# Twenty blocks of weight sums formed in the mixer, kept in DRAM, and read by the second feed-forward

## The chip, the core and the metric

The kernel runs on one core of one Trainium2 chip. The metric is the time of one execution on the device in microseconds (us); of several executions the median is taken. The engines are named as the profile names them: PE is TensorE (matrix products), with PEld its weight loads; DVE is VectorE; ACT is ScalarE; POOL is GpSimd; SP is SyncE, which computes nothing here and issues DMA transfers. A "q" behind a name (SPq, PEq) is that engine's instruction queue.

## The reference

One decoder layer over 256 tokens of width 2048 in float32: a feed-forward, a token mixer, a cross-attention into 256 memory rows, a second feed-forward, a final norm.

```python
def swiglu(h, w_gate, w_up, w_down):
    return (jax.nn.silu(h @ w_gate) * (h @ w_up)) @ w_down

for l in range(DEPTH):                                   # DEPTH = 1
    x = x + 0.5 * swiglu(rms_norm(x, ffn1_norm[l]), ffn1_w_gate[l], ffn1_w_up[l], ffn1_w_down[l])
    x = gated_parallel_mixer(x, mix_norm[l], w_in[l], ...)   # windowed attention beside RWKV-7
    x = memory_cross_attention(x, mem, cross_norm[l], ...)
    x = x + 0.5 * swiglu(rms_norm(x, ffn2_norm[l]), ffn2_w_gate[l], ffn2_w_up[l], ffn2_w_down[l])
return rms_norm(x, final_norm)
```

The weights of a feed-forward are 2048 x 5632 (gate, up) and 5632 x 2048 (down); each is read from DRAM once. The mixer's input projection is 2048 x 8992.

## The kernel before, in words

**Precision.** Each float32 operand is split into a high part `hi` (a rounding copy on ACT) and the rest `lo` (a subtraction on DVE). One product of 128 rows x 128 deep x 512 columns is then three matmuls on PE: hi x hi, hi x lo, lo x hi (`times`, lines 413 to 415 of the profile). Activations are split once; weights are split as they stream in, on lines 339 (`hi`) and 340 (`lo`) in `split_unit`.

**Order of the weights.** `weight_plan` lists all weights in the order of their use. A unit is two rows of 128 (KU = 2) by 512 columns of one weight, 512 KB. An item is what PE takes in one go: one unit, or, in the feed-forwards, a pair of units (gate and up, or two column blocks of down). In the feed-forwards one DMA brings two units of a weight (1 MB, tile `raw2`, four buffers); in the mixer each brings one (tile `raw`, four buffers). All weight loads are issued by SP, in order; a load waits on SP until the buffer that it overwrites has been read. `next_item` loads several units ahead and splits (`divide`) one pair, or two single units, ahead. `hi` and `lo` have three buffers each.

**Seven products.** A pair item multiplies two token halves by two weights over two rows of 128: eight products, 24 matmuls. For the pairs listed in `SEVEN` (pairs 0, 2, 4 of the eight in each column block of gate and up) a scheme of the Strassen and Winograd kind needs seven products, 21 matmuls. It needs sums: four of activations, made once (`combinations`), and four of weights, made for each such item in `sums`, by four subtractions on DVE (lines 350 to 353) from the raw gate and up units, and then split into `thi` (ACT, line 355) and `tlo` (DVE, line 356). `thi` and `tlo` hold all four sums and have one buffer. The four sums lie in two tiles from the `raw` ring until they are split. `product_pair` issues the seven products in the order p1, p2, p7, p6, p4, p3, p5; p6 and p7 go to PSUM banks `tr`, which the transposes share.

**Stages.** The first feed-forward (`feed_forward`, pool `f1`) runs to about 690 us of the profile, the mixer and the cross-attention (pool `mx`) to about 1545 us, the second feed-forward (pool `f2`) to the end. In each feed-forward the 11 column blocks of gate and up come in groups of 4, 4 and 3, each followed by its part of down. The first block of gate and up is plain; ten blocks use seven products. In the mixer, products with `w_in` (`product`) alternate on PE with small work: attention, decay, the recurrence (`pair`, with the masked products `mk` on line 1186) and its finish. That small work is written as Python generators in an `Interleave`; each `tick` of a product advances every group of them a step, so the program's text is woven together. A scheduler that runs when the program is built then fixes the order on each engine by its own estimate of times; on the chip each engine goes through its list in order.

**Where the mixer keeps things.** Most of its tiles share the ring `t4` (N4 = 20 buffers of 4 KB in each partition). The chunks of the recurrence run after the attention branch has been gated; at that point the weights of receptance and value and the second gate are multiplied.

The lines the change touches: the constants near the top, `feed_forward_plan`, the constants `bdup` and `center`, the building of `items`, `load`, `sums`, `divide`, `next_item`, `combinations`, `product_pair`, and the begin of the `mx` pool.

## Time and profile before

| | |
|---|---|
| median of 3 runs (lowest, highest) | 2269.42 us (2266.2, 2269.75) |
| the profiled execution, its own time | 2267.66 us |
| its span, first to last instruction | 2265.9 us |
| mean granted clock of TensorE | 0.999 |
| bytes moved by DMA | 432.75 MB, mean 191 GB/s |
| slices of 1/40 of the span: highest and lowest rate | 262 and 88 GB/s |

The profiled execution is one more execution, read by the hardware profiler. Busy time is the time in which an engine has at least one instruction in work; matmuls overlap, so a busy PE need not be at its full pace, and the distance from one matmul's start to the next says more. "Idle before" is the time an engine stood still before the instructions of a group, put down to whatever ended it. Idle time of an engine that is not the bottleneck costs nothing.

### The profile page before, as it was taken

How to read it: one execution, taken by the hardware profiler on the slowest of the kernel's cores; microseconds unless marked ns; L12 is line 12 of the kernel's file. 1: busy time of each engine (PE TensorE's matmuls, PEld its weight loads, DVE VectorE, ACT ScalarE, POOL GpSimd, SP SyncE). 2: the span in 40 equal slices, each digit the busy share in tenths (PEclk: the TensorE clock that was granted, in tenths of full speed). 3: DMA queues.
4: the chain of work that ended last, by engine and by line, in shares of the span. 5: the costliest groups of instructions: out<-in, count | busy, mean ns of one | idle time of the engine just before them, and what ended most of it. 6: DMA issues, size and time to landing. Idle time of an engine off the chain costs nothing.

```text
span 2265.9 us, 28100 instructions
## 1 busy us (share of the span) xinstructions
PE 2244.2 (99%) x10613; PEld 1840.5 (81%) x10613; DVE 1784.2 (79%) x2283; ACT 1230.7 (54%) x1655; POOL 134.1 (6%) x194
## 2 busy tenths in 40 slices
PE   9999999999999999999999999999999999999998
PEld 7888888888888877788888888888888888888886
DVE  7899989898988477895444556547899998998987
ACT  6555555555556477544444446556555555555554
POOL 1000000000001000201220021001000000000001
PEclk9999999999999999999999999999999999999999
DMA  7565565555556544676533486657555556556563
GB/s 262 186 206 200 189 212 196 186 204 205 187 195 203 164 134 140 195 229 208 150 88 93 154 262 228 195 168 262 202 187 205 203 198 210 186 188 220 186 212 141
DMA packets 219240, 432.75 MB, mean 191 GB/s; under 512 B 14140, under 2 KB 16417, under 8 KB 219105
## 3 DMA queue, kind: packets, MB, share of 16 engines
q1 hardware_dynamic: 210432, 404.78, 54.1%
q0 software_dynamic: 8208, 25.39, 3.5%
q8 instruction: 83, 1.36, 0.2%
q10 hardware_dynamic: 464, 0.79, 0.1%
q14 instruction: 53, 0.43, 0.1%
HBM read 417.56 MB, written 13.11 MB: 190 GB/s over the span
## 4 chain that ended last, share of the span: by engine, by line
PE 86%; DVE 5%; issue 4%; DMA 2%; ACT 2%; POOL 0%; SPq 0%; POOLq 0%; DVEq 0%; ACTq 0%
PE acc L413 17%; PE acc L414 17%; PE acc L415 17%; PE mm L414 7%; PE mm L415 7%; PE mm L413 7%; DVE lo L340 2%; PE tr L600 2%; PE tr L414 2%; PE tr L415 2%; PE tr L413 2%; PE mm L1212 1%; DMA raw<-in_ffn_w_down_dram 1%; PE tr L1181 1%; ACT hi L339 1%
## 5 line engine op out<-in xcount | busy, mean ns | idle before, releaser
L339 ACT CAST hi<-raw 128x1024 fp32r<-128x1024 f32 (+1 forms) x770 | 766.0, 997 | 731.1 <-PE acc L415 423.8
L340 DVE TENSOR_TENSOR lo<-raw,hi 128x1024 fp32r<-128x1024 f32 (+1 forms) x770 | 892.2, 1164 | 341.5 <-ACT hi L339 339.5
L413 PE MATMUL acc<-hi,xhi 128*128 128x512 f32 (+1 forms) x1196 | 476.9, 399 | 3.1 <-ACT xhi L627 2.5
L414 PE MATMUL acc<-lo,xhi 128*128 128x512 f32 (+1 forms) x1196 | 465.8, 389 | 2.2 <-DVE lo L340 2.0
L415 PE MATMUL acc<-hi,xlo 128*128 128x512 f32 (+1 forms) x1196 | 464.6, 389 | 0.0
L413 PEld LDWEIGHTS acc<-hi,xhi 128*128 128x128 f32 x1196 | 224.7, 188 | 52.5 <-issue 5.1
L414 PEld LDWEIGHTS acc<-lo,xhi 128*128 128x128 f32 x1196 | 224.9, 188 | 49.9 <-DVE lo L340 4.4
L415 PEld LDWEIGHTS acc<-hi,xlo 128*128 128x128 f32 x1196 | 224.4, 188 | 47.6 <-DVE xlo L628 1.0
L355 ACT CAST thi<-raw 128x1024 fp32r<-128x1024 f32 x172 | 180.4, 1051 | 102.3 <-DVE raw L351 55.1
L356 DVE TENSOR_TENSOR tlo<-raw,thi 128x1024 fp32r<-128x1024 f32 x172 | 208.9, 1221 | 4.5 <-ACT thi L355 4.5
L413 PE MATMUL mm<-hi,xhi 128*128 128x512 f32 x380 | 149.2, 393 | 0.0
L415 PE MATMUL mm<-hi,xlo 128*128 128x512 f32 x380 | 148.1, 390 | 0.0
L414 PE MATMUL mm<-lo,xhi 128*128 128x512 f32 x380 | 148.1, 390 | 0.0
L414 PE MATMUL acc<-lo,hhi 128*128 128x512 f32 x372 | 145.5, 391 | 0.4 <-DVE lo L340 0.4
L415 PE MATMUL acc<-hi,hlo 128*128 128x512 f32 x372 | 145.4, 391 | 0.0
L413 PE MATMUL acc<-hi,hhi 128*128 128x512 f32 x372 | 145.1, 390 | 0.0
L415 PEld LDWEIGHTS mm<-hi,xlo 128*128 128x128 f32 x380 | 71.3, 188 | 15.0
L413 PEld LDWEIGHTS mm<-hi,xhi 128*128 128x128 f32 x380 | 71.4, 188 | 14.5
L414 PEld LDWEIGHTS mm<-lo,xhi 128*128 128x128 f32 x380 | 71.4, 188 | 14.5
L414 PEld LDWEIGHTS acc<-lo,hhi 128*128 128x128 f32 x372 | 69.9, 188 | 14.9 <-DVE lo L340 0.8
L350 DVE TENSOR_TENSOR raw<-raw,raw 128x512 f32<-128x512 f32 x86 | 59.1, 688 | 28.9 <-DMA raw<-in_ffn_w_up_dram 23.7
L413 PEld LDWEIGHTS acc<-hi,hhi 128*128 128x128 f32 x372 | 69.8, 188 | 14.4
(386 smaller groups left out, 3559.1 us busy)
## 6 DMA issues: line engine op xcount, KB each, us to landing
raw<-in_ffn_w_up_dram SPq DMA_DIRECT2D x88, 1024.0 KB, 6.8
raw<-in_ffn_w_down_dram SPq DMA_DIRECT2D x88, 1024.0 KB, 5.5
raw<-in_ffn_w_gate_dram SPq DMA_DIRECT2D x84, 1024.0 KB, 5.3
raw<-in_w_in_dram SPq DMA_DIRECT2D x136, 512.0 KB, 3.8
raw<-in_w_out_dram SPq DMA_DIRECT2D x32, 512.0 KB, 4.7
raw<-in_w_proj_attn_dram SPq DMA_DIRECT2D x16, 512.0 KB, 3.6
raw<-in_w_proj_rwkv_dram SPq DMA_DIRECT2D x16, 512.0 KB, 5.7
raw<-in_w_cross_kv_dram SPq DMA_DIRECT2D x16, 512.0 KB, 3.7
```

Source lines behind the costliest of these rows:

```text
L339: at["hi"] = act.copy(hi[:, s], raw[:, s])
L340: at["lo"] = dve.tensor_tensor(lo[:, s], raw[:, s], f32(hi[:, s]), ALU.subtract)
L350: dve.tensor_tensor(ta[:, 0], ru[:, 0], rg[:, 0], ALU.subtract)
L355: act.copy(hi[:, 2 * i : 2 * i + 2], t[:])
L356: dve.tensor_tensor(lo[:, 2 * i : 2 * i + 2], t[:], f32(hi[:, 2 * i : 2 * i + 2]), ALU.subtract)
L413: pe.matmul(o, xh, hi, start=first, stop=False, **how)
L414: pe.matmul(o, xh, lo, start=False, stop=False, **how)
L415: pe.matmul(o, xl, hi, start=False, stop=last, **how)
L600: pe.transpose(b[:, o : o + P], tok[:, t, col : col + P], ident[:])
L1181: pe.matmul(b[e][:, m * P : (m + 1) * P], x1[r, j, cs_], x2[r, j, cs_], start=True, stop=True,)
L1212: pe.matmul(vb[:, o : o + P][:, r], lhs(e), rhs[:, r], start=first and e == 0, stop=True, **ek,)
```

## The change

1. In the second feed-forward, gate and up take seven products in pairs 0, 1, 2 and 4 of the ten column blocks (`SEVEN_2`), not 0, 2 and 4.
2. The sums of pairs 1 and 2 of those blocks (`STAGED`), 20 items, are not formed there. A new generator, `stage`, runs twice side by side in the mixer. For each item it loads the up and the gate unit by SP into two `t4` tiles, forms the four sums on DVE in place, and stores the two tiles by SP to the DRAM tile `sums_d`. The first four items come at the mixer's beginning (`STAGE_EARLY`); the other 16 after the mark "gated", at the recurrence.
3. `load_sums` brings the sums back into two `raw` tiles, asked for two items ahead. The row of up that is then not needed (`first_unused`) is left out of its load.
4. In both feed-forwards a seven item is split in another order: the first two sums, then gate, the second row of up, and the last two sums. The parts are now `thia`/`tloa` and `thib`/`tlob`, one buffer each. The order of products is now p7, p6, p1, p2, p3, p4, p5.
5. `bdup` and `center` move into the mixer's pool; N4 goes from 20 to 22.

```diff
-N4 = 20
+N4 = 22
+STAGE_EARLY = 4
 SEVEN, SEVEN_DOWN = (0, 2, 4), ((2, 4, 6), (2, 4))
+SEVEN_2, STAGED = (0, 1, 2, 4), (1, 2)
...
-                yield (wg, wu), 0, KD, (j * 512, j * 512), SEVEN
+                yield (wg, wu), 0, KD, (j * 512, j * 512), SEVEN_2 if last else SEVEN
...
+    bg.group("stage", 2)
...
-            items += [((u + i, u + 2 + i), (k - k0) // KU + i in n) for i in range(2)]
-    raws, parts = {}, {}
+            for i in range(2):
+                q = (k - k0) // KU + i
+                if n == SEVEN_2 and q in STAGED:
+                    staged[len(items)] = len(staged)
+                items.append(((u + i, u + 2 + i), q in n))
+    raws, parts, summed = {}, {}, {}
+    first_unused = {items[i][0][1] for i in staged}
+    sums_d = dram.tile([len(staged), P, 4, 512], F32, name="sums")
...
+        if u in first_unused:
+            second = u + 1 in first_unused
+            pieces = [(slice(1, 2), nc.sync)] + [(slice(2 + second, 4), nc.sync)]
+            if not second:
+                pieces = ((slice(1, 4), nc.sync),)
+        elif u + 1 in first_unused and wide:
+            pieces = ((slice(0, 2), nc.sync), (slice(3, 4), nc.sync))
...
+    def load_sums(i):
+        if i not in staged or i in summed:
+            return
+        summed[i] = [
+            wp.tile([P, KU, 512], F32, tag="raw", name="raw", bufs=4) for _ in range(2)
+        ]
+        for e, t in enumerate(summed[i]):
+            nc.sync.dma_start(t[:], sums_d[staged[i], :, KU * e : KU * e + KU, :])
+
+    def stage(t4, first):
+        yield from idle(8 * first)
+        for i, n in list(staged.items())[first::2]:
+            if n >= STAGE_EARLY:
+                yield from wait_for("gated")
+                yield from idle(8 * first * (n < STAGE_EARLY + 2))
+            t = t4("su", (P, KU, 512)), t4("sg", (P, KU, 512))
+            for e, v in zip(t, items[i][0][::-1]):
+                w, k, c0, _ = units[v]
+                rows = slice(k * P, (k + KU) * P)
+                nc.sync.dma_start(e[:], w[rows, c0 : c0 + 512].rearrange("(a p) n -> p a n", p=P))
+            yield from idle(7)
+            u0, u1, g0, g1 = (e[:, c] for e in t for c in range(KU))
+            with tc.issue_after(at["lo"].ins):
+                dve.tensor_tensor(g0, u0, g0, ALU.subtract)
+                dve.tensor_tensor(u0, u1, u0, ALU.subtract)
+            yield
+            with tc.issue_after(at["lo"].ins):
+                dve.tensor_tensor(u1, u1, g0, ALU.subtract)
+                dve.tensor_tensor(g1, g1, u1, ALU.subtract)
+            yield from idle(3)
+            for c, e in enumerate(t):
+                nc.sync.dma_start(sums_d[n, :, KU * c : KU * c + KU, :], e[:])
+            yield from idle(2)
...
-    def sums(g, u):
...
+    def two_parts(v, e):
+        sp = at["pool"]
+        hi = sp.tile([P, KU, 512], F32R, tag="thi" + e, name="thi")
+        lo = sp.tile([P, KU, 512], F32R, tag="tlo" + e, name="tlo")
+        act.copy(hi[:], v[:])
+        dve.tensor_tensor(lo[:], v[:], f32(hi[:]), ALU.subtract)
         return hi, lo
...
+        t = summed.get(i)
+        if t is None:
+            rg, ru = raws[g], raws[u]
+            t = [wp.tile([P, KU, 512], F32, tag="raw", name="raw", bufs=4) for _ in range(2)]
+            dve.tensor_tensor(t[1][:, 0], ru[:, 0], rg[:, 0], ALU.subtract)
+            dve.tensor_tensor(t[0][:, 0], ru[:, 1], ru[:, 0], ALU.subtract)
+            dve.tensor_tensor(t[0][:, 1], ru[:, 1], t[1][:, 0], ALU.subtract)
+            dve.tensor_tensor(t[1][:, 1], rg[:, 1], t[0][:, 1], ALU.subtract)
+        a_ = two_parts(t[0], "a")
+        parts[i] = split_unit(g), split_unit(u, slice(1, 2)), (a_, two_parts(t[1], "b"))
...
             for v in items[j][0]:
                 load(v)
+            load_sums(j)
             divide(j)
+        load_sums(i + 2)
         return parts[i]
...
+                ta, tb = s
                 for i, (to, x_, w_) in enumerate((
+                    ("p7", of_c(q, 2), of_w(ta, 0)), ("p6", of_c(q, 1), of_w(ta, 1)),
                     ("p1", of_x(0, k), of_w(g, 0)), ("p2", of_x(0, k + 1), of_w(g, 1)),
-                    ("p7", of_c(q, 2), of_w(s, 1)), ("p6", of_c(q, 1), of_w(s, 2)),
-                    ("p4", of_x(1, k + 1), of_w(s, 3)), ("p3", of_c(q, 3), of_w(u, 1)),
-                    ("p5", of_c(q, 0), of_w(s, 0)),
+                    ("p3", of_c(q, 3), of_w(u, 1)), ("p4", of_x(1, k + 1), of_w(tb, 1)),
+                    ("p5", of_c(q, 0), of_w(tb, 0)),
                 )):
...
+        for e in range(2):
+            bg.spawn("stage", stage(t4, e))
...
+        bg.seen.add("gated")
         for h in range(2):
```

More of the change, by code (lines that the diff above doesn't have):

```diff
@@ L206, in mixer_constants @@
         select(mask_l[:], ups, [[-1, P]], ALU.is_gt, 0.0, 0, 1)
+        bdup = sp.tile([P, P], F32, name="bdup")
+        center = sp.tile([P, P], F32, name="center")
         bdones = sp.tile([P, P], F32, name="bdones")
@@ L210, in mixer_constants @@
         pool.memset(bdmean[:], 0.0)
-        pool.memset(bdup, 0.0)
+        pool.memset(bdup[:], 0.0)
         for e in range(2):
@@ L292, in decoder_layer @@
     junk_t = cpool.tile([P, 512], mybir.dt.bfloat16, name="junk")
-    plan, units, items, ends = [], [], [], []
+    plan, units, items, ends, staged = [], [], [], [], {}
     for entry in weight_plan(a):
@@ L656, in feed_forward @@
                 ("hhi", [P, 16, T], F32R, 1), ("hlo", [P, 16, T], F32R, 1),
-                ("hb", [P, 2, 512], F32, 2), ("thi", [P, 4, 512], F32R, 1),
-                ("tlo", [P, 4, 512], F32R, 1),
+                ("hb", [P, 2, 512], F32, 2), ("thia", [P, KU, 512], F32R, 1),
+                ("tloa", [P, KU, 512], F32R, 1), ("thib", [P, KU, 512], F32R, 1),
+                ("tlob", [P, KU, 512], F32R, 1),
             ):
@@ L662, in feed_forward @@
         c = combinations(
-            sp, norm.x, SEVEN, "c", lambda: norm.r is not None and at["item"] > begun + 4
+            sp, norm.x, SEVEN_2 if last else SEVEN, "c", lambda: norm.r is not None and at["item"] > begun + 4
         )
```

35 lines of the change are left out of this document (10 added, 25 removed).

## The prediction

> **What bounds the kernel now.** I read the page's first part, then windows by stage, then TensorE's waits, and only then the engines beside it. First the span and the engines' shares:
>
> ```profile
> span 2265.9 us, 28100 instructions
> PE 2244.2 (99%) x10613; PEld 1840.5 (81%) x10613; DVE 1784.2 (79%) x2283; ACT 1230.7 (54%) x1655; POOL 134.1 (6%) x194
> ```
>
> PE is without work for 2265.9 - 2244.2 = 21.7 us. Next, windows: the burst at the start, the head of the mixer, the recurrence, the second feed-forward (columns: us, busy us of PE, PEld, DVE, ACT, POOL with counts, PE clock, DMA share, GB/s):
>
> ```profile
> 10.00:20.00 10.00, 9.13 (x45) 6.74 (x44) 6.90 (x11) 7.22 (x14) 0.00 (x0) 1.00 1.05 387
> 725.00:765.00 40.00, 40.00 (x183) 33.09 (x182) 19.26 (x21) 20.81 (x29) 5.52 (x20) 1.00 0.67 198
> 1014.00:1282.00 268.00, 267.59 (x1596) 222.24 (x1595) 129.87 (x157) 119.27 (x221) 41.70 (x66) 1.00 0.46 132
> 1545.00:2245.00 700.00, 699.61 (x3134) 577.31 (x3134) 629.08 (x782) 390.97 (x455) 16.26 (x17) 1.00 0.59 204
> ```
>
> In the second feed-forward PE lacks 0.4 us of 700, at full clock. Busy does not prove full pace, so two rows of PE's timeline there, the first and the last of 39 matmuls of 128x512 that follow each other:
>
> ```profile
> 1701.90 0.39 PE L413 MATMUL mm<-hi,chi 128*128 128x512 f32 x1
> 1710.52 0.39 PE L415 MATMUL acc<-hi,xlo 128*128 128x512 f32 x1
> ```
>
> (1710.52 - 1701.90) / 38 = 0.2268 us from start to start; the 0.39 us of one overlaps its neighbours. This is the price of a matmul here. The engines that feed PE, and PE's own waits on VectorE (groups: count | busy us, mean ns | idle before, by releaser; waits: total us, times, longest):
>
> ```profile
> L339 ACT CAST hi<-raw 128x1024 fp32r<-128x1024 f32 (+1 forms) x770 | 766.0, 997 | 731.1 <-PE acc L415 423.8 <-PE mm L415 226.8 <-issue 32.9
> L355 ACT CAST thi<-raw 128x1024 fp32r<-128x1024 f32 x172 | 180.4, 1051 | 102.3 <-DVE raw L351 55.1 <-DVE raw L353 46.8
> L340 DVE TENSOR_TENSOR lo<-raw,hi 128x1024 fp32r<-128x1024 f32 (+1 forms) x770 | 892.2, 1164 | 341.5 <-ACT hi L339 339.5
> L356 DVE TENSOR_TENSOR tlo<-raw,thi 128x1024 fp32r<-128x1024 f32 x172 | 208.9, 1221 | 4.5 <-ACT thi L355 4.5
> L350 DVE TENSOR_TENSOR raw<-raw,raw 128x512 f32<-128x512 f32 x86 | 59.1, 688 | 28.9 <-DMA raw<-in_ffn_w_up_dram 23.7 <-DMA raw<-in_ffn_w_down_dram 4.7
> PE acc L414 <- DVE lo L340: 2.3, 4, 1.3
> PE tr L414 <- DVE tlo L356: 1.6, 3, 0.8
> ```
>
> ScalarE's casts wait for PE to give `hi` buffers back (423.8 + 226.8 us), VectorE waits for ScalarE (339.5 us), and PE waits 2.3 + 1.6 us for VectorE in the whole run. So preparation is held back by buffers and stays ahead; PE's number of matmuls sets the time. VectorE is the close second: 629 of 700 us in the second feed-forward.
>
> **The change, part by part.** Terms are against the profiled execution, 2267.66 us (its span 2265.9 and 1.8 around it).
>
> *Matmuls.* In ten column blocks of the second feed-forward's gate and up, pair 1 goes from 8 products to 7, three matmuls each: 10 x 3 = 30 fewer. 30 x 0.2268 = 6.8 us, all on PE, which carries the path: -6.8. Ends: -6.8, and 0 if stalls fill the room.
>
> [...]
>
> *VectorE, second feed-forward.* Per block, pair 2 loses its four subtractions (4 x 0.688 = 2.75 us); pair 1 trades two `lo` (2 x 1.164) for one `lo`, half a `lo` (about 0.69, the 512-wide form) and two `tlo` (2 x 1.221): +1.96. Net -0.8 per block, -7.9 in ten. ScalarE gains two `thi` for half a `hi`, about +1.6 per block, on an engine busy 391 of 700 us. Both at nothing: what hides them is the PE time they run beside, and the saving buys none, since buffers hold this chain. Were that cover gone, VectorE's term would be a gain of up to 7.9.
>
> *Loads, second feed-forward.* 40 loads of 512 KB come, 20 rows of 256 KB go: 40 x 0.524 - 20 x 0.262 = 15.7 MB in 700 us, 22 GB/s on 204, against the 387 reached in the first window. A 512 KB load lands in about 4 us and a 1 MB one in 5 to 7:
>
> ```profile
> raw<-in_ffn_w_up_dram SPq DMA_DIRECT2D x88, 1024.0 KB, 6.8
> raw<-in_w_in_dram SPq DMA_DIRECT2D x136, 512.0 KB, 3.8
> x1d<-x POOLq DMA_DIRECT2D x4, 512.0 KB, 4.4
> ```
>
> The sums are asked for two items ahead, 2 x 21 x 0.2268 = 9.5 us, so 3.8 us + cast 1.05 + `tlo` 1.22 = 6.1 fits with 3.4 to spare; at 6.8 us landing, 0.4 remain. At nothing; ends 0 and, where each landing were late by the mean of the waits above (23.7 us over 28 of them, 0.85), 20 x 0.85 = 17.
>
> *Three sevens in a row.* Pairs 0, 1, 2 now follow each other, and the second half of the sums (`thib`, `tlob`) has one buffer. It is free when the last product of pair 0 is done; then cast 1.05 and `tlo` 1.22 = 2.3 us, needed before the sixth product of pair 1, 15 x 0.2268 = 3.4 us later. 1.1 us remain, twice a block. If one `lo` (1.16) stands in the way on VectorE, the miss is about 0.1; if also one cast (1.0), 1.1. I take +0.5 in all; ends 0 and 20 x 1.1 = 22, unlikely, as both would have to fall so each time.
>
> *The new order of the seven products, in both feed-forwards.* Products of the first half of the sums come first, so VectorE must finish three subtractions and one `tlo` first (3 x 0.688 + 1.22 = 3.3 us), and the last half only for the sixth; before, one `lo` started the item and both halves were wanted by the third and fourth product, after 1.16 + 2.75 + 2 x 1.22 = 6.4 us of VectorE, 9 matmuls (2.0 us) in: a lead of 4.3 against 3.3 now. The waits that this could remove are 1.6 us. At the 11 down passes that open with seven, PE's transposes stand just ahead, and the six matmuls (1.4 us) that covered the wait for a `tr` bank now come after. I take 0; ends -1.6 and 11 x 0.8 (the longest such wait) = 9.
>
> *The mixer.* 20 stagings, each two loads and two stores of 512 KB on SP, and four subtractions: 80 x 0.688 = 55 us on VectorE, 80 issues on SP. Four stagings fall at the mixer's head: 8.4 MB in some 40 us is 210 GB/s on 198, 21 over the 387: 40 x 21 / 387 = 2.2 us of transfers late, most of it taken up by four `raw` buffers. +0.5; ends 0 and 2.2. Sixteen run from the weights of the first receptance block on (1014 to 1282 us): 33.6 MB, 125 GB/s on 132, in all 257; VectorE 130 + 44 = 174 of 268. What could be held there:
>
> ```profile
> SPq L331 <- DVE lo L340: 218.0, 56, 10.9
> DVE lo L340 <- ACT hi L339: 89.2, 47, 5.2
> DVE mk L1186 <- PE tr L1181: 22.4, 12, 3.3
> PE tr L1195 <- DVE mk L1186: 0.2, 1, 0.2
> 1243.17 3.35 DVE L1276 RECIPROCAL sq<-sq 128x512 f32<-128x512 f32 x1 [0.68 <-ACT sq L1274]
> ```
>
> SP stands idle 218 of 268 us waiting for buffers, so its issues find room; behind a staged load that waits for a `t4` buffer, or a store that waits for VectorE, stand weight loads, and behind those the casts. VectorE already runs a reciprocal of 3.35 us here with no wait of PE behind it, longer than two subtractions (1.4). The thin edge is `mk`, which PE takes at once: VectorE is in a staged subtraction 44/268 = 16% of the time, rest of a pair on the mean 0.7 us, 16 chunks: 16 x 0.16 x 0.7 = 1.8 us if nothing covers it. +0.8; ends 0 and 1.8, not counting SP (a rival below).
>
> *The rest:* `bdup` and `center` are set on POOL, busy 6%; two more `t4` buffers; and, once, four sums of activations for pair 1 in place of two differences, three small VectorE operations beside the first column block. 0.
>
> Sum: -6.8 + 0.5 + 0 + 0.5 + 0.8 = -5.0, 2262.7 us. The median of the runs is 2269.42, 1.8 above the profiled one; the sum put there gives 2264.4. I forecast 2263, nearer the sum's own. 0.2% of 2269.42 is 4.5 us, about what a measurement tells from no change.
>
> **Rivals.**
>
> *SP's queue holds weight loads (slower).* Place: the mixer. A staging puts two waits on SP ahead of weight loads, 40 in all. For it: SP waits in order, and in the compiled order three stagings issue their loads only two or three weight units ahead of their subtractions. Against: the 218 us above, and `raw` loads that have four buffers of room. Price: 0.85 us a staging if PE pays what VectorE paid for a late load: 20 x 0.85 - 6.8 + 0.5 = +10.7, 2278; with half of them, 2270. It eats the gain from 6.8 / 20 = 0.34 us a staging, and is slower beyond measurement from (6.8 + 4.5) / 20 = 0.57. [...] Nothing in this trace shows stores on SP between loads. Chance 0.22; I give 2274.
>
> *The gain is half eaten (no change).* `thib` or late sums stall PE some 0.25 us at each of 20 staged items, 5 us: 2262.7 + 5 = 2268. For it: the margins of 0.4 and 1.1 us. Against: VectorE has 0.8 us less to do per block. Chance 0.20.
>
> *More than the matmuls.* The new order removes the 2.3 + 1.6 us that PE waits for VectorE and the mixer costs nothing: 2267.66 - 6.8 - 3.9 = 2257. For it: the smaller lead that an item asks for. Against: some of these waits are the kernel's start. Chance 0.10.
>
> **How the numbers follow.** The forecast has 0.48, with its own range 2260 to 2265. Faster: the forecast and the larger gain, 0.58, less 0.02 for its upper edge at 2265: 0.56. Within 0.2%: 0.20. Slower: the SP rival and its like at the item boundaries, 0.24. The range runs from 2256, just under the larger gain, to 2275, which takes in the SP rival up to 0.7 us a staging and leaves about 0.1 above.
>
> **What would show it.** In the second feed-forward, 30 fewer matmuls and PE idle still under 1 us of its window: the first term. A wait of PE on `tlo` of the second half, or of `thi` on a load of `sums`: the item boundaries. PE waiting for `lo` between 727 and 770 or 1014 and 1290 us, with SP waiting on VectorE's subtractions or on `t4` buffers just before: the SP rival. PE waiting on `mk`: the subtractions. More PE idle at the head of down passes: the order. The forecast is wrong if PE's idle time grows by over 2.3 us.

## The result and the profile after

The changed kernel takes 2277.69 us (median of 5 runs, 2274.97 to 2283.05), the one before 2267.45 (5 runs, 2266.2 to 2269.75): 1.0041 of before, 95% interval 1.003 to 1.0053. It is slower, by about 10 us, and lies above the range. The profiled execution is the one of 2277.83 us. Its page begins:

```profile
span 2276.0 us, 28433 instructions
PE 2247.5 (99%) x10583; PEld 1837.2 (81%) x10583; DVE 1830.2 (80%) x2346; ACT 1249.6 (55%) x1675; POOL 131.8 (6%) x194
```

The 30 matmuls are gone (10613 to 10583), and the span is 10.1 us longer all the same. To see where, I cut the span at TensorE's first matmul with a given weight, followed through the trace from the load over the cast to the matmul. Head is from the first product of `w_in` to that of `w_proj_attn`, recurrence from there to `w_proj_rwkv`, and so on; us:

```
                  ffn1    head   recur.  proj_rwkv  w_out  cross    ffn2    span
before           709.7   190.7    402.9       46.4   94.8  102.3   711.0  2265.9
after            707.2   200.5    410.1       46.4   96.1  102.3   705.5  2276.0
```

The second feed-forward gave 5.5 us and the first 2.5; the head of the mixer took 9.8 and the recurrence 7.2. Windows show how (columns: us, busy us and count of PE, PEld, DVE, ACT, POOL, then PE clock, DMA share, GB/s). Before:

```profile
725.00:790.00 65.00, 65.00 (x307) 54.20 (x306) 29.30 (x32) 32.98 (x44) 6.33 (x22) 1.00 0.60 173
1060.00:1120.00 60.00, 59.81 (x305) 48.87 (x303) 32.02 (x39) 25.23 (x33) 16.63 (x28) 1.00 0.63 176
1726.70:2265.90 539.20, 530.33 (x2366) 436.91 (x2364) 480.76 (x587) 291.17 (x332) 13.09 (x12) 0.99 0.56 193
```

After, the last row again from the first product of the second feed-forward's `down` to the end:

```profile
725.00:790.00 65.00, 61.20 (x266) 48.84 (x265) 35.24 (x42) 26.39 (x34) 5.16 (x23) 0.97 0.85 286
1060.00:1120.00 60.00, 57.03 (x267) 44.49 (x265) 44.28 (x58) 24.45 (x29) 10.30 (x16) 1.00 0.94 324
1740.90:2276.00 535.10, 525.96 (x2345) 432.98 (x2343) 477.01 (x573) 304.92 (x346) 13.49 (x12) 0.99 0.63 215
```

In the mixer the DMA engines' share goes from 0.60 to 0.85 and from 0.63 to 0.94, and PE, full before, lacks 3.8 and 3.0 us in these two windows. What stands behind it is read backwards through the waits (total us, times, longest). First SP's own in the changed kernel, the first three rows from 725 to 790 us, the last three from 1014 to 1300:

```profile
SPq L350 <- DVE lo L395: 19.4, 10, 5.4
SPq L385 <- DVE su L381: 13.0, 3, 6.7
SPq L385 <- DVE sg L382: 4.1, 4, 1.3
...
SPq L350 <- DVE lo L395: 133.8, 40, 9.9
SPq L385 <- DVE su L381: 47.6, 15, 9.1
SPq L385 <- DVE sg L382: 9.2, 15, 1.8
```

L385 is the store of a sum. It waits for VectorE up to 6.7 and 9.1 us, and the weight loads (L350) behind it wait too; SP's idle time for `lo`, its spare time, falls to 133.8 us from 232.0 in the same window before (the prediction's 218.0 is of a window 18 us shorter). Then the loads themselves, which land later (count, size, median us from issue to landing; 1014 to 1300 us), before:

```profile
raw<-in_w_in_dram SPq DMA_DIRECT2D x64, 512.0 KB, 3.7
```

and after, with the staging's own loads:

```profile
raw<-in_w_in_dram SPq DMA_DIRECT2D x60, 512.0 KB, 5.6
su<-in_ffn_w_up_dram SPq DMA_DIRECT2D x16, 512.0 KB, 6.8
```

ScalarE's waits in the changed kernel, 725 to 790 us first and 1014 to 1300 then, have rows that have no like in these windows of the kernel before:

```profile
ACT hi L394 <- DMA raw<-in_w_in_dram: 10.5, 5, 7.7
...
ACT hi L394 <- DMA raw<-in_w_in_dram: 22.2, 11, 4.8
```

and PE's waits over the whole run have grown for `lo` (2.3 before) and for `mk` (0.2 before), and are new for `hi`:

```profile
PE acc L472 <- DVE lo L395: 6.1, 11, 1.3
PE acc L471 <- ACT hi L394: 3.8, 4, 1.7
...
PE tr L1258 <- DVE mk L1249: 0.7, 2, 0.6
```

One instance in the head can be followed row by row, in the timelines of SP and ScalarE:

```profile
748.02 0.34 SPq L385 DMA_DIRECT2D sums<-su  x1
749.76 0.34 SPq L385 DMA_DIRECT2D sums<-sg  x1
751.55 1.02 SPq L350 DMA_DIRECT2D raw<-in_w_in_dram  x2
758.82 1.04 ACT L394 CAST hi<-raw 128x1024 fp32r<-128x1024 f32 x1 [7.71 <-DMA raw<-in_w_in_dram]
```

SP stands at the store of `su` for 6.7 us and at that of `sg` for 1.3. The first weight load behind them goes out at 751.55 us, behind two loads of the next staging, and lands 7.2 us later. The cast has waited 7.71 us for it, and PE's wait for that cast ends at 759.91, in the first of the timelines below. So the chain is: a store waits for VectorE on SP, the weight loads behind it go out late and in a bunch, at a time when the staging's transfers fill the DMA engines; the cast waits for its load, `lo` for the cast, PE for both. How much of the lateness is the waiting and how much the full DMA engines, this trace alone does not say.

PE's idle time is not the whole price. In the recurrence it grows from 1.7 to 5.2 us, and PE's busy time grows as much, from 401.1 to 404.9 us for the same 2213 matmuls at full clock: after a late operand matmuls start further apart, and the profile counts part of that as busy. At 1105.93 us, for one, the matmul that waits 0.53 us for `lo` starts 0.93 us behind the one before it, and the next 0.34 us behind it, where 0.23 is usual: 0.81 us late, of which 0.53 count as idle. In the head the clock comes into it too. PE's timeline there:

```profile
757.79 0.39 PE L473 MATMUL acc<-hi,xlo 128*128 128x512 f32 x1
759.91 0.73 PE L471 MATMUL acc<-hi,xhi 128*128 128x512 f32 x2 [1.74 <-ACT hi L394]
761.17 0.50 PE L472 MATMUL acc<-lo,xhi 128*128 128x512 f32 x1 [0.53 <-DVE lo L395]
```

and windows there, cut to two steps of the granted clock:

```profile
758.50:761.90 3.40, 1.46 (x5) 0.94 (x6) 1.93 (x2) 2.09 (x2) 0.00 (x0) 1.00 1.03 392
761.90:765.30 3.40, 3.40 (x10) 2.65 (x9) 0.52 (x1) 0.00 (x0) 0.00 (x0) 0.50 1.05 372
```

PE waits 1.74 and 0.53 us for `hi` and `lo`, is busy 1.46 of 3.40 us, and has the next 3.41 us at half the clock. In such a step matmuls start 0.43 us apart in place of 0.23, so it does little over half its work: an estimated 1.6 us lost. The changed kernel's trace has three in the mixer (at 761.9, 799.4, 867.7 us), some 4.8 us of the head's 9.8; the trace before has none until the last 6 us of the span. In the clock record of the changed kernel's trace each of the three is 3.413 us long, at 0.50 of full speed.

### The profile page after: what moved, and what is told of

Same layout as the page of the kernel before. It is cut to its first block, busy times and chain, and to the rows that moved or that the text cites. A ratio compares the mean times of both kernels' runs of the same rounds, so it can differ in the third digit from the quotient of the medians.

```text
span 2276.0 us, 28433 instructions
## 1 busy us (share of the span) xinstructions
PE 2247.5 (99%) x10583; PEld 1837.2 (81%) x10583; DVE 1830.2 (80%) x2346; ACT 1249.6 (55%) x1675; POOL 131.8 (6%) x194
## 4 chain that ended last, share of the span: by engine, by line
PE 86%; DVE 4%; issue 4%; DMA 3%; ACT 1%; POOL 0%; SPq 0%; POOLq 0%; ACTq 0%; DVEq 0%
PE acc L471 17%; PE acc L472 17%; PE acc L473 16%; PE mm L473 8%; PE mm L472 8%; PE mm L471 8%; PE tr L472 2%; PE tr L659 2%; PE tr L473 2%; PE tr L471 2%; DMA raw<-in_w_in_dram 2%; DVE lo L395 1%; PE mm L1275 1%; PE tr L1244 1%; ACT hi L394 1%
## 5 line engine op out<-in xcount | busy, mean ns | idle before, releaser
L394 ACT CAST hi<-raw 128x1024 fp32r<-128x1024 f32 (+1 forms) x770 | 756.1, 992 | 731.6 <-PE acc L473 479.8
L471 PE MATMUL acc<-hi,xhi 128*128 128x512 f32 (+1 forms) x1166 | 465.0, 400 | 6.4 <-ACT hi L394 3.8
L472 PE MATMUL acc<-lo,xhi 128*128 128x512 f32 (+1 forms) x1166 | 457.0, 392 | 5.3 <-DVE lo L395 5.3
L473 PE MATMUL acc<-hi,xlo 128*128 128x512 f32 (+1 forms) x1166 | 454.5, 390 | 0.0
L471 PEld LDWEIGHTS acc<-hi,xhi 128*128 128x128 f32 x1166 | 219.6, 189 | 57.1 <-ACT hi L394 6.6
L403 DVE TENSOR_TENSOR tlo<-raw,thi 128x1024 fp32r<-128x1024 f32 x192 | 232.5, 1220 | 3.5 <-ACT thi L402 0.4
L402 ACT CAST thi<-raw 128x1024 fp32r<-128x1024 f32 x192 | 200.2, 1051 | 60.5 <-DVE raw L425 38.7
L473 PEld LDWEIGHTS acc<-hi,hlo 128*128 128x128 f32 x372 | 70.0, 188 | 14.0
```

The source lines that it names most:

```text
L394: at["hi"] = act.copy(hi[:, s], raw[:, s])
L402: act.copy(hi[:], v[:])
L403: dve.tensor_tensor(lo[:], v[:], f32(hi[:]), ALU.subtract)
L471: pe.matmul(o, xh, hi, start=first, stop=False, **how)
L472: pe.matmul(o, xh, lo, start=False, stop=False, **how)
L473: pe.matmul(o, xl, hi, start=False, stop=last, **how)
```

## The experiments

Two questions: which term of the sum was wrong, and what of the staging costs the time. Theory H: a store that waits for VectorE holds the weight loads behind it on SP's queue. Theory R: the transfers lie too dense, however they are queued. Theory D: VectorE's subtractions delay the `lo` parts. All ratios are against the kernel before, run beside each on the same chip (medians 2268.4 to 2269.2). The stretches of all profiled executions, in the columns above, follow. Each row is a single execution and holds its half-clock steps; that of stores_pool, 2267.42 us, was 2.3 us under the kernel's median:

```
                  ffn1    head   recur.  proj_rwkv  w_out  cross    ffn2    span
order_only       707.4   190.8    403.1       46.4   96.3  102.4   712.1  2266.4
no_stage         707.4   193.5    405.4       46.4   96.5  102.3   723.5  2282.9
early0           707.2   191.6    415.3       56.5   96.2  102.3   706.8  2283.9
stores_pool      707.2   192.3    408.4       46.4   95.7  102.3   705.3  2265.6
late_store       707.2   194.1    402.2       53.1   95.2  102.3   706.3  2268.4
nosubs_pool      707.3   199.3    408.3       46.4   96.5  102.3   706.3  2274.3
one_pool         707.2   192.6    403.6       58.8  101.8  102.3   705.4  2279.8
all_pool         707.2   195.9    410.1       46.4   95.6  102.3   706.5  2271.7
paced_hold       707.3   191.8    404.3       58.0   96.2  102.3   705.8  2273.6
late13           707.4   193.2    405.8       46.4   96.3  102.3   706.1  2265.4
half0            707.1   193.6    403.0       46.4   96.5  102.3   708.2  2265.1
mix14            707.3   193.4    403.1       46.4   96.2  102.4   708.1  2264.9
```

**The order of the products alone (order_only).** Three sevens as before in the second feed-forward, no stagings; the new order of the seven products stays.

```diff
-                yield (wg, wu), 0, KD, (j * 512, j * 512), SEVEN_2 if last else SEVEN
+                yield (wg, wu), 0, KD, (j * 512, j * 512), SEVEN
...
-            sp, norm.x, SEVEN_2 if last else SEVEN, "c", lambda: norm.r is not None and at["item"] > begun + 4
+            sp, norm.x, SEVEN, "c", lambda: norm.r is not None and at["item"] > begun + 4
```

(Here and in no_stage the tile `sums_d` is kept with one row that nothing uses.)

> Leaves out the staging and the fourth pair of sevens; keeps the new order of the seven products and of their preparation, the two halves of thi and tlo with a buffer each, the moved constants and 22 t4 buffers. My reading of the two profiles is that the first feed-forward gained 2.7 us by the order alone (the mixer's first product starts at 715.1 us and not at 717.8) and that the mixer lost 18 us by the staging. Theory A (the order helps both feed-forwards, the staging carries the whole loss): 2262 to 2264 us, 4 to 5 below the kernel before, a mixer as long as before (about 837 us from its first product to the first of the second feed-forward), and a clock at half only at the end. Theory B (the order is worth nothing, the 2.7 us are chance): 2267 to 2268 us. Theory C (the moved constants or the two more t4 buffers cost part of the mixer's loss): 2265 us or more with a mixer over 840 us.

Measured: 2268.76 us (11 runs, 2267.36 to 2272.9), 1.0003 of before, 0.9994 to 1.0011. The order is worth nothing in sum, but not nowhere. The first feed-forward is 2.3 us shorter, 2.2 of it in its passes of `down`: PE's three waits for `tlo` in the prediction's row, 1.6 us, all lay in that feed-forward and are gone. The second is 1.1 longer, and the products of `w_out` 1.5 longer, for causes that I did not follow. So theory A was right on the first feed-forward and wrong on the time, and theory C was not excluded: the moved constants and the two more buffers are in this run as well.

**The seven products without the stored sums (no_stage).** All four sums are formed on the spot in the second feed-forward; nothing is staged.

```diff
-SEVEN_2, STAGED = (0, 1, 2, 4), (1, 2)
+SEVEN_2, STAGED = (0, 1, 2, 4), ()
```

> Four pairs of sevens in the second feed-forward, but no staging: all sums are formed there by VectorE. Per column block VectorE gets 4.7 us more than in the kernel before (pair 1: two tlo, one lo, half a lo and four subtractions in place of two lo), 47 us in ten, on 629 busy of 700. Theory A (buffers hold the preparation and PE's count sets the time; staging buys nothing): 6.8 us below order_only, about 2256 to 2258 us. Theory B (VectorE is full there and becomes the bound, so the sums have to be formed elsewhere): PE waits for tlo in the second feed-forward, VectorE's busy time comes to 98% of the blocks, and the time is above order_only by up to 47 - 71 + 6.8 and more where the work is not spread evenly, 2264 to 2280 us.

Measured: 2281.24 us (5 runs, 2280.93 to 2284.59), 1.0058, 1.0046 to 1.007. The second feed-forward is 12.5 us longer than before, with the 30 matmuls gone. Its window from `down`'s first product on:

```profile
1733.90:2282.80 548.90, 530.47 (x2345) 431.70 (x2343) 506.04 (x629) 304.31 (x346) 13.49 (x12) 0.99 0.56 190
```

and PE's longest wait from `gate` on:

```profile
PE tr L471 <- ACT thi L402: 11.3, 11, 1.4
```

VectorE does 506 us there (477 in the changed kernel, 480.76 before), and 667.04 in the whole of that feed-forward (625.80 in the changed kernel). PE waits 11.3 us for the parts of the sums, as theory B said. With no sums stored the fourth seven does not pay; staging can't simply go.

**All stagings in the recurrence (early0).**

```diff
-STAGE_EARLY = 4
+STAGE_EARLY = 0
```

> All 20 stagings after the mark at the recurrence, none at the mixer's head. At the head the changed kernel lost 9.8 us from the mixer's first product to the first of the attention projection (200.5 us against 190.7), among them three steps of 3.4 us at half clock. Theory A (the four early stagings cause all of that): the head is back at about 191 us with the clock full there, and the four stagings moved to the recurrence add 4/16 of the 7.3 us lost there: 2277.7 - 9.8 + 1.8 = 2269.7 us. Theory B (the head is slow for another reason, such as the layout of the mixer's tiles): no change, 2277 us or more.

Measured: 2285.97 us (5 runs, 2285.83 to 2290.04), 1.0082, 1.0069 to 1.0095. The head is back at 191.6, so the four early stagings cost the head its time. But the recurrence grows by 5.2 us over the changed kernel's, and the stagings that now run on beside `w_proj_rwkv` make that stretch 56.5 in place of 46.4, so the time is 16 us over the 2269.7 that I had expected. It is not a matter of the head: where the stagings are this dense, time is lost.

**The stores on another queue (stores_pool).**

```diff
-                nc.sync.dma_start(sums_d[n, :, KU * c : KU * c + KU, :], e[:])
+                pool.dma_start(sums_d[n, :, KU * c : KU * c + KU, :], e[:])
```

> The stores of the sums are issued by GpSimd's queue; their place in the program, their number and bytes are the same. Theory A (weight loads stand on SP behind stores that wait for VectorE's subtractions: SP waits 47.6 + 9.2 us there between 1014 and 1300 us): most of the mixer's loss goes, at the head and at the recurrence: 18.3 us less two thirds, 2263 to 2268 us, with SP waiting for lo as in the kernel before. Theory B (the 42 MB of loads and 42 MB of stores and loads back fill the DMA engines, busy share 0.94 between 1060 and 1120 us, and loads land late whoever issues them): 2275 to 2279 us, and loads of w_in land after 6 to 9 us as now. Theory C (VectorE's subtractions are in the way of lo and mk): as B in time, but with PE's waits on mk and lo and loads landing sooner.

Measured: 2269.7 us (12 runs, 2266.74 to 2281.5), 1.0012, 0.9999 to 1.0025. One line takes back 8 of the 10 us, somewhat less than theory A said. It is the head that is cured (192.3); the recurrence is 408.4, 5.5 over before. Its windows in the recurrence:

```profile
1020.00:1060.00 40.00, 40.00 (x182) 33.12 (x181) 28.62 (x34) 17.60 (x19) 6.19 (x10) 1.00 0.96 331
1060.00:1100.00 40.00, 37.91 (x176) 30.29 (x175) 31.36 (x38) 17.63 (x21) 8.65 (x13) 1.00 0.99 352
1100.00:1140.00 40.00, 38.08 (x244) 30.81 (x243) 24.91 (x36) 13.59 (x32) 18.02 (x30) 1.00 0.93 290
```

**Late stores on SP (late_store).** The same queue as in the changed kernel, but the store comes ten steps behind the subtractions.

```diff
-            yield from idle(3)
+            yield from idle(10)
             for c, e in enumerate(t):
```

> The two stores of a staging stay on SP's queue, but are issued seven steps later, when VectorE has formed the sums. Theory H (a store that waits for VectorE holds the weight loads behind it): SP's waits for su and sg (70 us in the recurrence and 17 in the head of the mixer in the changed kernel) are nearly gone, the head of the mixer comes to 192-194 us (200.5 changed, 190.7 before), the stretch with the recurrence to 407-409 (410.1, 402.9), and the time to 2268-2271. Theory V (not the waiting, but that the queue has 80 more transfers in line, or the volume): nothing moves, head 198-201, recurrence 409-411, 2275-2279.

Measured: 2270.45 us (11 runs, 2268.2 to 2273.24), 1.0005, 0.9996 to 1.0014. The recurrence is 402.2, no longer than before and better than either theory said, with all its stores on SP, though only 12 of the 16 later stagings store their sums in it. What it loses is 6.7 us at `w_proj_rwkv`, which the other four now reach. That is a new wait, of PE on a VectorE multiply with the gate that POOL's queue loads (PE's waits, 1300 to 1380 us):

```profile
PE acc L471 <- DVE gl L1397: 4.7, 2, 2.9
```

A window of late_store over that stretch:

```profile
1311.00:1364.00 53.00, 48.30 (x218) 39.21 (x217) 38.65 (x45) 20.42 (x23) 14.57 (x14) 0.97 1.02 364
```

The DMA share is 1.02 there; over the same products of the kernel before it was 0.83:

```profile
1311.00:1357.00 46.00, 46.00 (x216) 38.10 (x215) 27.56 (x29) 20.65 (x23) 15.27 (x14) 1.00 0.83 273
```

This run changed two things at once, since a staging takes 20 steps in place of 13, so the transfers are also spread wider; two further runs part these.

**Spread wider, but still waiting (paced_hold).** The seven steps go behind the stores.

```diff
                 nc.sync.dma_start(sums_d[n, :, KU * c : KU * c + KU, :], e[:])
-            yield from idle(2)
+            yield from idle(9)
```

> Stores on SP's queue three steps after the subtractions, as in the changed kernel, so that they still wait for VectorE; the seven steps more that the kernel with late stores has come behind the stores, so that a staging takes 20 steps as there, in place of 13. Theory H (the waiting stores hold the weights): the recurrence's stretch stays long, 406-410 (late stores 402.2, changed 410.1, before 402.9), SP's waits for su and sg stay above 30 us, time 2271-2277. Theory R (it is how dense the transfers lie): as with late stores, 402-404 and 2268-2271. In both the stagings run on into proj_rwkv and that stretch is 50-54 us.

Measured: 2275.9 us (6 runs, 2274.12 to 2278.93), 1.0031, 1.002 to 1.0043. `w_proj_rwkv` is 58.0, 11.6 over before and more than either theory allowed. The recurrence is 404.3, near theory R's range, again with 12 of the 16 stagings in it.

**As dense, but waiting less (late13).** Still 13 steps a staging.

```diff
-            yield from idle(7)
+            yield from idle(5)
             u0, u1, g0, g1 = (e[:, c] for e in t for c in range(KU))
...
-            yield from idle(3)
+            yield from idle(6)
             for c, e in enumerate(t):
...
-            yield from idle(2)
+            yield from idle(1)
```

> Stores on SP's queue later behind the subtractions (six steps in place of three), the loads' lead shortened from seven steps to five and the pause behind the stores from two to one: 13 steps for a staging as in the changed kernel, so the density of transfers is the changed kernel's and the stagings end before proj_rwkv. Theory H: head 191-194, recurrence 402-405, proj_rwkv 46.4, time 2261-2266, less than before's 2268-2269. Theory R: recurrence 407-410, time 2268-2274. Another way: the subtractions now wait for loads that have not landed, VectorE's line with them, and PE waits for lo: 406-412.

Measured: 2268.2 us (11 runs, 2266.65 to 2273.19), 1.0002, 0.9993 to 1.0011. The recurrence is 405.8, between the two theories' ranges, with all 16 stagings in it. SP's waits on the subtractions from 1014 to 1300 us in late_store:

```profile
SPq L385 <- DVE sg L382: 4.6, 4, 2.0
SPq L385 <- DVE su L381: 3.2, 6, 1.1
```

in paced_hold:

```profile
SPq L385 <- DVE su L381: 25.3, 10, 7.1
SPq L385 <- DVE sg L382: 7.9, 11, 1.9
```

and in late13:

```profile
SPq L385 <- DVE su L381: 20.6, 16, 3.7
SPq L385 <- DVE sg L382: 12.2, 16, 3.6
```

Of the changed kernel's 7.2 us in the recurrence, paced_hold is rid of 5.8, late13 of 4.3, late_store of 7.9. These are not clean shares of R and H. In paced_hold and late_store four stagings have left the stretch and cost their time at `w_proj_rwkv`. And paced_hold's waits on the subtractions fell as well, from 56.8 to 33.2 us, about late13's 32.8. Clearer are the 120 us in which most stagings fall. In the changed kernel, late13, paced_hold and late_store:

```profile
1020.00:1140.00 120.00, 116.28 (x562) 93.33 (x561) 84.97 (x104) 49.71 (x66) 21.15 (x31) 1.00 0.96 321
1020.00:1140.00 120.00, 118.22 (x612) 96.72 (x610) 84.94 (x108) 49.97 (x72) 25.48 (x35) 1.00 0.95 332
1020.00:1140.00 120.00, 119.73 (x631) 98.44 (x630) 79.49 (x98) 49.89 (x73) 23.08 (x35) 1.00 0.86 278
1020.00:1140.00 120.00, 119.82 (x631) 98.77 (x631) 80.53 (x99) 50.94 (x74) 23.12 (x35) 1.00 0.87 280
```

Where the transfers are spread (0.86 and 0.87), PE loses next to nothing, in paced_hold with stores that still wait up to 5.1 us in this window. Where they are dense, it loses 3.7 us in the changed kernel, 1.8 in late13, and 4.0 in stores_pool, in which no store stands on SP. So theory R is borne out for the recurrence. Theory H is not excluded there, since late13 does better at the same density, but late13 also moved the loads and the pauses, and is no clean test.

**Without the subtractions (nosubs_pool).** Stores on GpSimd's queue; the four subtractions are left out, so what is stored is not the sums.

```diff
-            with tc.issue_after(at["lo"].ins):
-                dve.tensor_tensor(g0, u0, g0, ALU.subtract)
-                dve.tensor_tensor(u0, u1, u0, ALU.subtract)
             yield
-            with tc.issue_after(at["lo"].ins):
-                dve.tensor_tensor(u1, u1, g0, ALU.subtract)
-                dve.tensor_tensor(g1, g1, u1, ALU.subtract)
```

> Stores on GpSimd's queue, and VectorE's four subtractions of a staging left out (the tiles are stored as they were loaded, so the computation is changed: the two later pairs of feed forward 2's gate and up get wrong sums). With the stores on GpSimd's queue the recurrence's stretch was still 5.5 us longer than before (408.4). Theory R (what is left is the transfers: the DMA engines were 0.93-0.99 busy from 1020 to 1140 us): the stretch stays at 407-409, time 2266-2270. Theory D (what is left is the 64 subtractions on VectorE ahead of the lo parts): the stretch comes to 403-404, the head to 191, time 2261-2265.

Measured: 2275.1 us (9 runs, 2272.54 to 2279.2), 1.0026, 1.0016 to 1.0035: not faster than with them (the intervals overlap). The recurrence stays at 408.3, so nothing speaks for theory D. The run does not exclude it: the stores no longer wait for VectorE and go out earlier, into the loads, which can hide what the missing subtractions save:

```profile
1020.00:1060.00 40.00, 38.59 (x171) 31.16 (x170) 22.34 (x20) 16.84 (x20) 5.14 (x9) 1.00 1.01 354
1060.00:1100.00 40.00, 39.01 (x177) 31.86 (x176) 21.01 (x27) 16.35 (x18) 10.99 (x16) 1.00 1.00 355
```

The DMA engines are full, at 354 and 355 GB/s, and the head is 199.3, 7.0 over stores_pool's. The trace has three half-clock steps between 748 and 804 us. So in the head, too, dense transfers alone, with no store on SP, can cost about what the changed kernel loses.

**One staging at a time (one_pool).** Stores on GpSimd's queue as in stores_pool.

```diff
-    bg.group("stage", 2)
+    bg.group("stage", 1)
...
-        for i, n in list(staged.items())[first::2]:
+        for i, n in list(staged.items()):
...
-        for e in range(2):
-            bg.spawn("stage", stage(t4, e))
+        bg.spawn("stage", stage(t4, 0))
```

> Stores on GpSimd's queue, and one staging at a time in place of two, so that the 16 later ones go on until the products of w_out. Theory R (transfers too dense): DMA share from 1020 to 1140 us falls from 0.96 to about 0.8, the recurrence's stretch to 403-405 (408.4 with two), the stretches of proj_rwkv and w_out stay within 1 us, time 2262-2266, which would be less than before's 2268. Theory D (subtractions): half of them still lie in the stretch, 405-407, time 2266-2268. A third way: the stagings late in w_out and proj_rwkv cost there what they save, 2268-2271.

Measured: 2281.49 us (5 runs, 2278.0 to 2282.54), 1.0052, 1.0039 to 1.0064. The recurrence is 403.6, as R said. The loss is moved: `w_proj_rwkv` 58.8 and `w_out` 101.8, 12.4 and 7.0 over before. The third way that I named was right in kind, and far too small in size.

**The staging's loads on GpSimd's queue too (all_pool).**

```diff
-                nc.sync.dma_start(e[:], w[rows, c0 : c0 + 512].rearrange("(a p) n -> p a n", p=P))
+                pool.dma_start(e[:], w[rows, c0 : c0 + 512].rearrange("(a p) n -> p a n", p=P))
```

beside stores_pool's edit.

> Both the loads and the stores of the stagings on GpSimd's queue, so that SP's has the weights alone. Theory H extended (the loads of a staging that wait for a free buffer hold the weights too, some 5 us of waits on SP): the stretch of the recurrence 405-407, time 2264-2268. Theory R: 407-409 and 2267-2270, as with the stores alone moved. Another way: GpSimd's queue now holds its own transfers (xb, rb and others) behind loads that wait, the stretch grows past 409 and the time past 2271.

Measured: 2273.59 us (11 runs, 2268.53 to 2276.12), 1.0017, 1.0008 to 1.0026. SP has the weights to itself and the recurrence is 410.1, as long as in the changed kernel. PE's longest waits of the mixer, in all_pool:

```profile
PE acc L472 <- DVE lo L395: 5.7, 6, 2.5
PE tr L659 <- ACT tok L845: 4.6, 3, 3.4
```

Time and stretch are those of the third way, but the trace shows another mechanism for its longest wait, 3.4 us at 1105.5 us. The cast `tok` stands on ScalarE behind casts of weights, and these weights, which SP issued from 1087 to 1093 us, landed 10 to 14 us later; the DMA engines' share from 1060 to 1100 us is 1.02. Weights come late here with nothing else on their queue.

**Ten sums, all in the recurrence (half0).** On late_store: the third pair is formed on the spot as before, only the second is staged.

```diff
-STAGE_EARLY = 4
+STAGE_EARLY = 0
...
-SEVEN_2, STAGED = (0, 1, 2, 4), (1, 2)
+SEVEN_2, STAGED = (0, 1, 2, 4), (1,)
...
-            yield from idle(3)
+            yield from idle(10)
             for c, e in enumerate(t):
```

> Ten sums in place of 20: of the four pairs with seven products in feed forward 2's gate and up the second (1) is staged and the third (2) is formed on the spot as before; none of the stagings in the head of the mixer, all in the recurrence at 20 steps each, with late stores. Feed forward 2 keeps its saving if VectorE forms three of four sums there in time as it did before: gate and up to down end 5 us less than before (before 813.3 us from its first product to the end). Theory R and theory H both: head 190.7-192, recurrence 402-404, proj_rwkv 46.4, time 2261-2265. If VectorE does not keep up in feed forward 2 (three of four pairs and the split of 28 KB more), that part gains 0-2 only and the time is 2266-2269.

(The 813.3 us there count from the first product of the cross attention's weights; from `gate` on it is 711.0.) Measured: 2265.72 us (11 runs, 2263.19 to 2270.05), 0.9986, 0.9977 to 0.9995. The recurrence is 403.0 and `w_proj_rwkv` 46.4: ten stagings at this spacing cost nothing. The time is just above the range, with a half-clock step in the head that I had not expected. The second feed-forward gives 2.8 us of the 5.5, its VectorE at 490.65 us from `down`'s first product on:

```profile
1727.60:2265.00 537.40, 527.52 (x2345) 432.36 (x2343) 490.65 (x601) 304.67 (x346) 13.47 (x12) 0.99 0.60 204
```

**Fourteen sums (mix14).** On late_store, with four stagings in the head.

```diff
-                if n == SEVEN_2 and q in STAGED:
+                if n == SEVEN_2 and (q == 1 or q == 2 and len(staged) < 8):
```

> Late stores on SP's queue, 20 steps a staging, with 14 sums: the second pair (1) is always staged, the third (2) only in the first four of the ten column blocks and formed on the spot in the other six. Four stagings in the head of the mixer, ten in the recurrence, all done before proj_rwkv. Theory R and H: head 190.7-192.5, recurrence 402-403.5, proj_rwkv 46.4, feed forward 2 between the kernel with ten sums (3 less than before) and the one with 20 (5.6 less): 809 us from gate's first product to the end, time 2262-2266, 0.9975-0.999 of before. If the four in the head cost again what they did in the changed kernel (10 us), the time is 2272.

Measured: 2265.15 us (11 runs, 2261.79 to 2267.94), 0.9984, 0.9975 to 0.9993. It is below both kernels, the one before by 4.0 us (2269.16 beside it) and the changed one by some 12, and it can't be told from half0. The four stagings in the head cost nothing here (193.4, and 193.6 in half0, which has none there). The four more sums bought nothing in the second feed-forward (708.1, and 708.2).

In both, the head is still some 2.8 us over before. Windows of mix14 there:

```profile
787.70:791.10 3.40, 1.80 (x14) 1.45 (x14) 1.52 (x2) 0.68 (x2) 0.27 (x1) 1.00 0.91 223
791.10:797.90 6.80, 6.80 (x29) 5.50 (x30) 5.20 (x13) 1.72 (x2) 0.00 (x0) 0.50 0.27 88
```

6.8 us at half the clock, some 3.2 us lost, behind a wait for the keys (780 to 800 us), which every kernel here has:

```profile
PE mm L893 <- DMA kd<-kd: 1.6, 1, 1.6
```

Before, that wait had no such step in the profiled run:

```profile
791.10:797.90 6.80, 5.32 (x38) 4.17 (x37) 4.81 (x12) 1.72 (x3) 0.00 (x0) 1.00 0.63 178
```

## Why the prediction was wrong

*Matmuls, -6.8.* Right in mechanism, nearly in size. The second feed-forward fell by 5.5 us. From order_only the new order alone adds 1.1 there, so the 30 matmuls gave 6.6. PE's waits there are 0.8 us for `lo`, 0.4 before.

*VectorE and loads of the second feed-forward, 0; three sevens in a row, +0.5.* Right: no wait of PE on `tlo` of the second half or on a load of `sums` stands in that stretch. That VectorE's saving buys nothing was right for the changed kernel; no_stage shows how near the edge it lies, since 41 us more of VectorE there (667.04 against 625.80) made that feed-forward 18 us longer (723.5 against 705.5).

*The order, 0.* Right in sum (+0.5 us of span, the interval includes no change), and made of -2.3, +1.1 and +1.5 in three places. The end of -1.6 that the sum named is what came in the first feed-forward: all three waits for `tlo` lay there and went, and a wait costs more than its idle time. What the order costs in the other two places stays open.

*The mixer, +0.5 and +0.8.* This is the step that failed: it measured +9.8 and +7.2, 17.0 us. The 0.8 was the price of `mk` behind a subtraction, and PE's wait on `mk` did grow, but in that row from 0.2 to 0.7 us. What came instead is weights that land late, and that cost was put at nothing: for SP with the words "not counting SP", for the DMA engines by mean rates. The argument on SP was that it stands idle for 218 of 268 us. A mean idle time says little of a queue on which weight loads stand behind a store that waits (the 6.7 us ahead of 748.02): SP was idle *because* it was ahead. Four `raw` buffers hold work for PE of some 4 x 12 x 0.2268 = 10.9 us (an estimate, at 12 matmuls a unit), and one wait of 9.1 us of a store uses up most of that lead. The argument on the DMA engines was a mean of 257 GB/s from 1014 to 1282 us. The mean came true, 252, but the stagings are not spread over that stretch: it was 321 GB/s at 0.96 of the engines' time from 1020 to 1140, and 197 afterwards. And the 0.5 for the head set 210 + 198 GB/s against 387 as though late transfers could be caught up in the buffers; where PE waited there, the DMA engines were at 1.03, 392 GB/s.

*The rival.* The SP rival named the place and the signs: PE waits for `lo` and `hi`, SP on VectorE's subtractions just before. It is not the whole of what happened, since with no store on SP and transfers as dense the recurrence stays 5.4 to 7.2 us over before (nosubs_pool, stores_pool, all_pool), and nosubs_pool's head 8.6. Its price, 0.85 us a staging, agrees with 17.0 / 20 = 0.85 by luck: the four stagings in the head cost 2.45 us each, half of it half-clock steps, the 16 later ones 0.45. The price itself was misread, as the 23.7 us were 22 waits and not 28, 1.08 us each. With -5.5 in the second feed-forward, -2.5 in the first and +1.3 at `w_out` the 17.0 make +10.3, against the 10.1 of the spans. I gave the rival a chance of 0.22 on the strength of the idle time, and the range ended at 2275, below the 2278 that its full price made.

Moving the stores to GpSimd's queue took 2277.69 to 2269.7 us; but late13 and late_store do as well on the one queue (2268.2, 2270.45), where the store only comes later, and all_pool, with the staging's loads on GpSimd's queue too, is worse (2273.59). What the faster runs have in common is that no store waits long at the front of the weights' queue or that the transfers are spread.

## What to carry to other kernels

A store queued ahead of loads did better here when it was issued with its data ready or nearly so, not when they were asked for (late_store 2270.45 us and late13 2268.2, against 2277.69; neither moved the stores alone). Look at what the queue's longest single wait, here 9.1 us, does to the loads behind it, not at the queue's idle sum, here 133.8. Work moved into an "idle" stretch has to be held against the DMA engines where it falls, not against the mean of the stretch. Here 120 us at a share of 0.95 or 0.96 cost PE 1.8 to 4.0 us and at 0.85 to 0.87 at most 0.5. A short full piece is no loss by itself: from 1060 to 1100 us late_store and half0 have a share of 0.99 and PE is busy for all 40 us. Ten stagings in the recurrence at the wider spacing cost nothing; no run shows that of 16, which at this spacing reach the next stretch and cost 7 to 12 us there. Where the precomputed part has a cheap alternative on an engine with some room, half of the precomputation can be worth more than all of it (2265.72 us with ten sums, 2277.69 with 20).

## What was not expected of the hardware

A wait of PE of 1 to 2 us can cost more than itself. Where PE is busy for about half of a 3.41 us step or less (1.46 of 3.40 and 1.80 of 3.40 above), the clock of the next step, or two, can be 0.50, and an estimated 1.6 us of work are lost per step. It does not follow each time: the wait for the keys near 791 us gave a step of 6.8 us in some profiles and none in others of kernels that are alike up to there.

The clock records say more on when it does. In every trace with more than one half-clock step these begin whole multiples of 3.413 us apart (in the changed kernel's 799.417 is 11 such steps behind 761.871, and 867.684 another 20), so each of the 14 traces can be cut on a grid that runs through its half-clock steps. In the changed kernel's, PE is busy for 0.42, 0.51 and 0.73 of the three stretches ahead of its half-clock steps; three others, with 0.59, 0.62 and 0.59 (from 744.8, 877.9 and 1082.7 us), have none behind them. Over all 14, from 690 to 1570 us, there are 13 stretches of the grid, at full clock, in which PE is busy for half of the time or less, and a half-clock step follows each of them. Of 32 with a busy share of 0.51 to 0.64 it follows 8, of 30 with 0.65 to 0.73 one, and of some 3490 busier ones none. The wait for the keys left PE busy for 0.53 of its stretch in mix14, and a step followed; in order_only, with a wait of 1.4 us, 0.58, and none did.

The spread of a kernel's own times goes with the clock: of stores_pool's runs that of 2266.74 us had a mean granted clock of 0.999, that of 2281.5 one of 0.993, which by estimate is 0.006 x 2275 = 14 us, nearly all of the difference. That late weights lie behind the longer times is likely but not shown, as none of those executions was profiled.
